# Two quarters of w loaded as f32 by SyncE's queue at the head of a matmul with batch normalization

## The chip, the cores and the metric

The kernel runs on one core of a Trainium2 chip. A core has TensorE for matmuls (PE in the profile, its weight loads PEld), VectorE (DVE), ScalarE (ACT), GpSimd (POOL) and SyncE (SP), and 16 DMA engines that serve the queues of all of them. The metric is the device time of one execution in microseconds. The kernel before took 205.82 us (median of three runs, 205.68 to 205.83).

## The reference

```python
batch, m, k, n = 16, 512, 1024, 768          # x: (16, 512, 1024), weight: (1024, 768), f32
y = np.matmul(x, weight)
mean = np.mean(y, axis=(0, 1), keepdims=True)
var = np.var(y, axis=(0, 1), keepdims=True)
y_norm = (y - mean) / np.sqrt(var + eps)
return (gamma * y_norm + beta).astype(np.float32)
```

A product of 8192 x 1024 by 1024 x 768, and then each of the 768 columns is normalized with its mean and variance over all 8192 rows. No column can be written before all rows of it have been multiplied.

## The kernel before, in words

The 8192 rows of x are 16 chunks of 512 (CH); a chunk is two pieces of 256 rows (QR). The 1024 of the contraction are four blocks jw of 256, and each block holds two (e = 0, 1) sets of 128. The 768 columns are six groups nt of 128; the first two are computed with rows on the partitions (rows_unit, matmul L510: x is the stationary operand), the other four with columns on the partitions (col_unit, matmul L575: w is the stationary operand).

x and w are f32 in HBM and bf16 in the matmuls. In the kernel before, both are cast on the way by GpSimd's DMA queue: load_x (L395, its DMA at L403) brings 256 or 512 rows into the tile "ring" in four DMAs, one for each 32 partitions; load_quarter (L386, L387) brings 32 partitions of w, for two blocks jw at once, into w_sb. A "quarter" i is such a group of 32 partitions; "the first pair of blocks" is jw 0 and 1, the second jw 2 and 3. VectorE then turns x in 32 x 32 squares (turn_x, L435 and L428) into xT_sb, which comes from the pool xtpool with 12 buffers.

The order of the loads is the list at L440: x's first 256 rows, w's first pair, x's second 256 rows, w's second pair, then the rest of x. BETWEEN (L262) moves two quarters of w's first pair ahead of x's first DMA (L401 and L402), so the queue of GpSimd runs: w quarters 0 and 1, x's first 256 rows (four DMAs), w quarters 2 and 3, x's second 256 rows, w's second pair, x further. A DMA of GpSimd's queue waits until the one eight places before it has landed, since eight semaphores go round.

At the very head SyncE's queue issues four tiny DMAs ("touched", L350), each of which reads one f32 word of 64 rows of w, for the four quarters of the first pair. Nothing computes with what they bring.

TensorE begins with WAKE = 8 f32 matmuls of 128 x 512 on a tile of zeros (wake, L587, matmul L591; each is two passes in the profile) and eight small ones (L594). Then it computes the first chunk in parts (part, L774, called at L780 to L787): with the first pair of blocks on the first 256 rows (8 matmuls L510 and 16 matmuls L575), one idle matmul (FILL = 1, L781 and L782), with the first pair on the second 256 rows, and then with the second pair on all 512 rows. The second chunk's rows follow.

All this work is written as tasks with an engine, an estimated duration and a due time; arrange (L122) plays them through with a model of the DMA queues (Wires, L98, whose field "free" is when the wires first come free) and gives the order in which each engine's instructions are emitted. Instructions emitted ahead of it, such as the four tiny DMAs, stand first in the order of their engine.

Of the kernel before, what the change touches and what calls it, by code (L numbers as in the profile page):

```python
# [97 lines left out]
class Wires:  # L98
# [2 lines left out]
    LANES = 8  # L101

    def __init__(self):
        self.free = 4.3
        self.lanes = {"SP": [], "POOL": [], "ACT": []}

    def ready(self, queue):
# [120 lines left out]
def kernel(  # L228
# [9 lines left out]
    nc = tc.nc  # L238
    f32 = mybir.dt.float32
# [5 lines left out]
    Kw, N = weight.shape  # L245
    assert K == Kw
    M = B * M0
    P = 128
# [6 lines left out]
    QPC = CH // QR  # L255
    JW = KQ // 64
    PIECES = ((0,QR),(QR,QR))
    WAKE = 8
    FILL = 1
    SMALL = 8  # L260
    TOUCH = 1
    BETWEEN = {0: [0, 1]}  # L262
    EARLY = 4
    SHORT = 2
    GA = 2
# [27 lines left out]
    def seq(bi):  # L293

        ins = bi.ins
        prev = last.get(ins.engine)
        if prev is not None:
            tc.add_manual_dep(
                ins, prev,
                mybir.DependencyInfo(mybir.DependencyClass.NoSync, mybir.DependencyReason.DATA),  # L300
                reason="order",
            )
        last[ins.engine] = ins.name
        return bi
# [39 lines left out]
    fss = singles.tile([P, 2], f32)  # L344

    seq(nc.scalar.activation(warm, eps_sb, AF.Sqrt))
    touched = singles.tile([P, 2, TOUCH], f32)
    first_rows = weight.rearrange("(i jw c e) n -> i c jw (e n)", i=4, jw=JW, e=2)
    for i in range(4):
        seq(nc.sync.dma_start(touched[32 * i:32 * i + 32, 0:2], first_rows[i, :, 0:2, 0:TOUCH]))  # L350


    tasks, turns = [], {}
# [93 lines left out]
    affine = None  # L447
    for kind, n, *n1 in order:
        if kind == "w":
            quarters = [i for i in range(4) if n > 0 or i not in sum(BETWEEN.values(), [])]  # L450
            took = len(quarters) * 192 * 4 * (n1[0] - n) / 4 * PER_KB * 1.024
            w_ready[n] = task(t, {"POOL": (0.535 * len(quarters), 0.535 * len(quarters))}, load_w(n, *n1, quarters), dma=took)
            w_ready[n].count = len(quarters)
            t += 2.1 * (n1[0] - n)
            if n1[0] == JW:
                idt = task(t, {"POOL": (0.6, 0.6)}, lambda eng: make_identity(nc, ident))
                task(t, act(0.25), lambda eng: seq(nc.scalar.copy(ident32, ident)), [idt])
            continue
# [319 lines left out]
            col_unit(nt, 0, jws, q0, q1)  # L778

    part(0, 1, [0, 1])  # L780
    fill_slot = Slot(banks)  # L781
    pe_task(0.87 * FILL, wake(FILL, fill_slot), [w_ready[0]], takes=[fill_slot])  # L782
    part(1, 2, [0, 1])
    for h in range(2):
        rows_unit(0, [2 * h, 2 * h + 1], [2, 3])
# [626 lines left out]
```

## Time and profile before

| What | Value |
|---|---|
| Time, median of three runs | 205.82 us |
| Span of the profiled execution, first to last instruction (the page gives no other time of it) | 204.07 us |
| Mean granted TensorE clock | 0.979 |
| Busy: PE, PEld, DVE, ACT, POOL | 189.3, 114.5, 159.3, 146.2, 124.1 us |
| First matmul with data | 12.14 us after the span's start |
| Last matmul of the product (L753) | ends at 186.6 us |
| Read from HBM, written to it | 36.7 MB, 25.2 MB |

The profile's page divides the span into 40 slices, one digit for the busy tenths of each engine in each. A view of waits sums, for each engine and line, the idle time ahead of an instruction and names what ended it. A view in order of time lists instructions with start and length in microseconds; an entry "x4" stands for four instructions merged. DMA issues have the engine name with a q ("SPq") or the engine's own name (POOL). Under a DMA instruction's tile names, "ring<-in_x_dram" is a load of x, "w_sb<-in_weight_dram" one of w. In the DMA part, q0 "software_dynamic" is GpSimd's queue and q1 "hardware_dynamic" that of SyncE. From issue to landing the eight DMAs of w take 6.2 us in the median, those of x's first pieces 5.9, the four tiny ones 2.6.

### The profile page before, as it was taken

How to read it: one execution, taken by the hardware profiler on the slowest of the kernel's cores; microseconds unless marked ns; L12 is line 12 of the kernel's file. 1: busy time of each engine (PE TensorE's matmuls, PEld its weight loads, DVE VectorE, ACT ScalarE, POOL GpSimd, SP SyncE). 2: the span in 40 equal slices, each digit the busy share in tenths (PEclk: the TensorE clock that was granted, in tenths of full speed). 3: DMA queues.
4: the chain of work that ended last, by engine and by line, in shares of the span. 5: the costliest groups of instructions: out<-in, count | busy, mean ns of one | idle time of the engine just before them, and what ended most of it. 6: DMA issues, size and time to landing. Idle time of an engine off the chain costs nothing.

```text
span 204.1 us, 3510 instructions
## 1 busy us (share of the span) xinstructions
PE 189.3 (93%) x1210; PEld 114.5 (56%) x1210; DVE 159.3 (78%) x250; ACT 146.2 (72%) x260; POOL 124.1 (61%) x150
## 2 busy tenths in 40 slices
PE   7969999999999999999999999999999999997900
PEld 3457554657488888777865444444444445544600
DVE  4031879999999999969989998987999878657900
ACT  2001461368989999899978766999998959956950
POOL 7776954877499989997403999389613312940000
PEclk9999999999999999999999999999999999999965
DMA  4999999999999999999686899899999999999998
GB/s 71 172 199 196 176 196 196 196 197 197 190 193 197 197 196 196 196 197 195 103 181 200 297 339 336 248 301 328 295 322 227 336 303 274 347 343 310 310 347 253
DMA packets 98562, 48.74 MB, mean 239 GB/s; under 512 B 24304, under 2 KB 98032, under 8 KB 98544
## 3 DMA queue, kind: packets, MB, share of 16 engines
q0 software_dynamic: 34624, 18.36, 65.5%
q1 hardware_dynamic: 63920, 30.16, 52.6%
q8 instruction: 9, 0.15, 0.3%
q14 instruction: 9, 0.07, 0.1%
HBM read 36.71 MB, written 25.17 MB: 303 GB/s over the span
## 4 chain that ended last, share of the span: by engine, by line
PE 86%; ACT 3%; DMA 3%; POOL 2%; issue 1%; ACTq 0%; DVE 0%; POOLq 0%
PE y_ps L575 54%; PE y_ps L510 24%; PE y_ps L814 4%; ACT o_sb L1361 3%; DMA ring<-in_x_dram 3%; PE o_ps L1044 1%; POOL ring L403 1%; POOL w_sb L387 1%; PE y_ps L753 1%; PE a_ps L903 1%; PE o_ps L1074 0%; ACTq L1407 0%; PE idle_ps L591 0%; PE tot_ps L871 0%; ACT ring L1252 0%
## 5 line engine op out<-in xcount | busy, mean ns | idle before, releaser
L575 PEld LDWEIGHTS <-w_sb 128*128 128x128 bf16 x520 | 50.3, 97 | 57.6
L575 PE MATMUL y_ps<-xT_sb,w_sb 128*128 128x512 bf16 (+1 forms) x272 | 59.3, 371 | 0.0
L575 PE MATMUL y_ps<-x_pl,w_sb 128*128 128x512 bf16 x248 | 57.4, 379 | 0.0
L403 POOL DMA_DIRECT2D ring<-in_x_dram x76 | 47.2, 626 | 14.4 <-DMA ring<-in_x_dram 5.5
L510 PE MATMUL y_ps<-w_sb,xT_sb 128*128 128x256 bf16 x448 | 50.6, 273 | 1.7 <-DMA ring<-in_x_dram 1.6
L510 PEld LDWEIGHTS <-xT_sb 128*128 128x128 bf16 x448 | 43.5, 98 | 9.4 <-DVE xT_sb L435 2.9
L435 DVE STREAM_TRANSPOSE xT_sb<-ring 128x1024 f32<-128x1024 f32 (+1 forms) x29 | 31.2, 1111 | 14.1 <-DMA ring<-in_x_dram 13.9
L711 DVE BATCH_NORM_STATS2 stats<-y_ps 128x6 f32<-128x512 f32 x46 | 30.9, 687 | 7.7 <-PE y_ps L575 7.2
L715 ACT CAST y_sb<-y_ps 128x512 bf16<-128x512 f32 x51 | 29.0, 593 | 10.4 <-DVE stats L711 6.3
L547 ACT COPY x_pl<-xT_sb 128x1024 bf16<-128x1024 bf16 x32 | 32.8, 1063 | 1.7 <-DVE xT_sb L435 1.7
L942 POOL TENSOR_TENSOR ring<-ring,sum 128x1024 f32<-128x1024 f32 (+1 forms) x11 | 23.8, 2188 | 14.9 <-ACT y_ps L724 10.9
L659 ACT ACTIVATE sq_sb<-y_ps 128x512 f32<-128x512 f32 x28 | 16.3, 610 | 16.2 <-PE y_ps L510 15.9
L666 POOL TENSOR_TENSOR sum<-sum,sq_sb 128x512 f32<-128x512 f32 x20 | 25.6, 1278 | 3.0 <-ACT sq_sb L659 1.7
L662 DVE TENSOR_TENSOR sum<-y_ps,sum 128x512 f32<-128x512 f32 x28 | 18.9, 675 | 6.3 <-ACT sq_sb L659 5.3
L672 ACT CAST y_sb<-y_ps 128x512 bf16<-128x512 f32 x28 | 16.3, 594 | 8.2 <-DVE sum L662 8.0
L1178 POOL TENSOR_TENSOR ring<-ring,sum 128x1024 f32<-128x1024 f32 x6 | 14.8, 2477 | 9.8 <-issue 8.5
L937 DVE TENSOR_TENSOR ring<-y_sb,a_ps 128x1024 f32<-128x1024 bf16 (+1 forms) x16 | 16.7, 1079 | 0.1
L1044 PE MATMUL o_ps<-ident,y_sb 128*128 128x128 bf16 x104 | 13.1, 221 | 1.6 <-DVE y_sb L1348 1.5
L1232 ACT CAST ring<-ring 128x1024 f32<-128x1024 bf16 x13 | 13.8, 1063 | 0.6 <-DMA ring<-y_sb 0.6
L1145 POOL COPY sum<-sum 32x256 f32<-32x256 f32 (+1 forms) x17 | 5.8, 340 | 13.4 <-DVE sum L1142 6.5
L428 DVE STREAM_TRANSPOSE xT_sb<-ring 128x2048 bf16<-128x2048 bf16 x6 | 13.5, 2290 | 0.1
L591 PE MATMUL idle_ps<-idle_sb 128*128 128x512 f32 x18 | 9.6, 688 | 1.5 <-DVE idle_sb L316 1.5
(104 smaller groups left out, 153.7 us busy)
## 6 DMA issues: line engine op xcount, KB each, us to landing
out_dram<-ring SPq DMA_DIRECT2D x37, 512.0 KB, 3.4
ring<-in_x_dram POOLq DMA_DIRECT2D x52, 256.0 KB, 8.8
out_dram<-o_sb SPq DMA_DIRECT2D x6, 512.0 KB, 4.7
ring<-in_x_dram POOLq DMA_DIRECT2D x16, 128.0 KB, 5.9
w_sb<-in_weight_dram POOLq DMA_DIRECT2D x8, 192.0 KB, 6.2
out_dram<-ring SPq DMA_DIRECT2D x6, 256.0 KB, 3.0
ring<-in_x_dram POOLq DMA_DIRECT2D x4, 192.0 KB, 7.8
out_dram<-o_sb SPq DMA_DIRECT2D x3, 256.0 KB, 2.5
```

Source lines behind the costliest of these rows:

```text
L403: bi = seq(nc.gpsimd.dma_start(x_bf[32 * i:32 * i + 32], src[:, :, KQ * i:KQ * (i + 1)]))
L435: seq(nc.vector.transpose(dst, src[:, :, jw0:jw1]))
L510: seq(nc.tensor.matmul(y_ps[:, s], x_of(c, jw, e, t * P, (t + 1) * P), w_sb[:, jw, e, 0:NA], start=(s == 0 and jw == 0 and e == 0), stop=( ...
L547: seq(nc.scalar.copy(dst, pairs) if eng == "ACT" else ENG[eng].tensor_copy(dst, pairs))
L575: seq(nc.tensor.matmul(y_ps, w_sb[:, jw, e, nt * P:(nt + 1) * P], moving(c, jw, e, q0 * QR, q1 * QR, parted), start=(jw == 0 and e == 0 an ...
L659: seq(nc.scalar.activation(sq_sb[:, 0:n], slot.tile[:, 0:n], AF.Square))
L662: seq(nc.vector.tensor_add(sum1, slot.tile[:, 0:n], sum1))
L666: seq(ENG[eng].tensor_add(acc, acc, state["sq"][:, 0:n]))
L711: seq(nc.vector.bn_stats(dst, slot.tile))
L715: seq(nc.scalar.copy(y(nt, c), slot.tile))
L937: seq(nc.vector.tensor_mul(slot.o, y_row[c].y[:, s0:s1], aff[0][:, None, :].to_broadcast([P, n, NA])))
L942: seq(ENG[eng].tensor_add(slot.o, slot.o, row[:, None, :].to_broadcast([P, n, NA])))
```

## The change

SyncE's queue now loads quarters 0 and 1 of w's first pair as f32, in four DMAs of 192 KB (two quarters by two blocks jw), into two tiles from xtpool. VectorE casts block 0 of both quarters into w_sb (64 partitions x 1536 elements), ScalarE block 1. These six instructions take the place of the four tiny DMAs, ahead of everything that the planner orders on these engines but behind the memsets on VectorE and the table load on ScalarE. GpSimd's queue no longer loads these two quarters and starts with x's first rows. The idle matmuls at the head are six instead of eight, the one between the two first parts is gone, and the planner's model has its wires free at 3.6 instead of 4.3.

```diff
@@ class Wires
     def __init__(self):
-        self.free = 4.3
+        self.free = 3.6
@@ constants
-    WAKE = 8
-    FILL = 1
+    WAKE = 6
+    FILL = 0
     SMALL = 8
-    TOUCH = 1
-    BETWEEN = {0: [0, 1]}
+    AHEAD = (0, 1)
+    BETWEEN = {}
@@ ahead of the planned work
-    touched = singles.tile([P, 2, TOUCH], f32)
-    first_rows = weight.rearrange("(i jw c e) n -> i c jw (e n)", i=4, jw=JW, e=2)
-    for i in range(4):
-        seq(nc.sync.dma_start(touched[32 * i:32 * i + 32, 0:2], first_rows[i, :, 0:2, 0:TOUCH]))
+    ahead = [xtpool.tile([P, 2, N], f32, tag="xT", name=f"ahead{jw}") for jw in range(2)]
+    w_words = weight.rearrange("(i jw c e) n -> i c jw e n", i=4, jw=JW, e=2)
+    for i in AHEAD:
+        for jw in range(2):
+            seq(nc.sync.dma_start(ahead[jw][32 * i:32 * i + 32], w_words[i, :, jw]))
+    near = slice(32 * AHEAD[0], 32 * AHEAD[-1] + 32)
+    seq(nc.vector.tensor_copy(w_sb[near, 0], ahead[0][near]))
+    seq(nc.scalar.copy(w_sb[near, 1], ahead[1][near]))
@@ the loads of w
-            quarters = [i for i in range(4) if n > 0 or i not in sum(BETWEEN.values(), [])]
+            quarters = [i for i in range(4) if n > 0 or i not in AHEAD]
@@ the first parts
     part(0, 1, [0, 1])
-    fill_slot = Slot(banks)
-    pe_task(0.87 * FILL, wake(FILL, fill_slot), [w_ready[0]], takes=[fill_slot])
+    if FILL:
+        fill_slot = Slot(banks)
+        pe_task(0.87 * FILL, wake(FILL, fill_slot), [w_ready[0]], takes=[fill_slot])
     part(1, 2, [0, 1])
```

The order of instructions on each engine is otherwise the same in both kernels, with one exception on GpSimd: two small instructions that build the identity stand between other DMAs than before.

## Prediction

> **What bounds the kernel now.** I read the busy row of TensorE by slices first, then its waits, then the order of time of the first 26 us, then what the DMA queues moved there.
>
> ```profile
> span 204.1 us, 3510 instructions
> ...
> PE   7969999999999999999999999999999999997900
> ...
> PEclk9999999999999999999999999999999999999965
> ```
>
> TensorE is busy at nine tenths or more from the fifth of 40 slices to the 37th. Its waits, all of them:
>
> ```profile
> PE y_ps L510 <- DMA ring<-in_x_dram: 1.6, 1, 1.6
> PE o_ps L1044 <- DVE y_sb L1348: 1.5, 1, 1.5
> PE idle_ps L591 <- DVE idle_sb L316: 1.5, 1, 1.5
> ```
>
> Between the wait at the head and the one at the tail TensorE never stands idle, so what moves the head earlier moves the end by as much, if the loads come earlier too. The head in order of time (start, length, engine, line, count, idle before):
>
> ```profile
> 0.74 1.81 SPq L350 DMA_DIRECT2D touched<-in_weight_dram  x4
> 1.30 1.21 POOL L387 DMA_DIRECT2D w_sb<-in_weight_dram  x2 [0.85 <-POOLq L1393]
> 1.49 8.63 PE L591 MATMUL idle_ps<-idle_sb 128*128 128x512 f32 x16 [1.49 <-DVE idle_sb L316]
> 2.51 2.29 POOL L403 DMA_DIRECT2D ring<-in_x_dram  x4
> 4.79 1.06 POOL L387 DMA_DIRECT2D w_sb<-in_weight_dram  x2
> 10.26 1.30 DVE L435 STREAM_TRANSPOSE xT_sb<-ring 128x512 f32<-128x512 f32 x2 [7.13 <-DMA ring<-in_x_dram]
> 12.14 1.03 PE L510 MATMUL y_ps<-w_sb,xT_sb 128*128 128x256 bf16 x8 [1.58 <-DMA ring<-in_x_dram]
> 14.83 1.02 PE L591 MATMUL idle_ps<-idle_sb 128*128 128x512 f32 x2
> 14.85 1.30 DVE L435 STREAM_TRANSPOSE xT_sb<-ring 128x512 f32<-128x512 f32 x2 [3.28 <-DMA ring<-in_x_dram]
> ...
> 18.61 1.91 PE L510 MATMUL y_ps<-w_sb,xT_sb 128*128 128x256 bf16 x16
> ...
> 24.62 1.25 DVE L435 STREAM_TRANSPOSE xT_sb<-ring 128x1024 f32<-128x1024 f32 x1 [0.69 <-DMA ring<-in_x_dram]
> ```
>
> Beside these lines I put the trace's semaphore records, which tell when the last of a transfer's 16 parts landed. w's quarters 0 and 1: 4.99 and 6.02. The four parts of x's first 256 rows: 8.09, 8.77, 9.51, 10.14. w's quarters 2 and 3: 11.06 and 12.00. x's second 256 rows: 14.73 (last part). w's second pair of blocks: 18.47. x's fourth 256 rows: 24.50. So TensorE begins four times at a landing: at 12.14 (0.14 after w's quarter 3; the turn of x, done by about 11.0 for the half needed, had been there), at 15.85 (x turned by 15.5, then the tail of the idle matmul), at 18.61 (landing 18.47, and TensorE itself free at 18.53), at 25.93 (landing 24.50, turn to 25.87, TensorE free at 25.89). The name "ring" in the wait of 1.58 is that of a later transfer on the same semaphores.
>
> The stream itself is what these landings wait for. In the first 2.6 us only the hardware queue moved anything (packets, MB, share of 16 engines):
>
> ```profile
> q1 hardware_dynamic: 160, 0.00, 3.2%
> ```
>
> and afterwards the DMA engines are full except in one stretch (columns: length, busy time of PE, PEld, DVE, ACT, POOL, granted clock, DMA share, GB/s):
>
> ```profile
> 5.00:6.00 1.00, 1.00 (x3) 0.38 (x2) 0.00 (x0) 0.00 (x0) 1.00 (x4) 1.00 1.15 152
> 6.00:7.00 1.00, 1.00 (x4) 0.43 (x3) 0.00 (x0) 0.00 (x1) 0.92 (x4) 1.00 0.82 91
> 8.00:9.00 1.00, 1.00 (x3) 0.38 (x2) 0.00 (x0) 0.00 (x0) 0.57 (x1) 1.00 1.37 206
> ```
>
> Against 206 GB/s the two stretches before lost 0.26 + 0.56 us, and 7 to 8 (180 GB/s) another 0.13: about 0.95 us soon after x is first read.
>
> **The change, part by part.** The order of the instructions on each engine is the same in both kernels but for what follows.
>
> *Start of the stream.* SP's first DMA is issued at 0.74 and its first packet runs at 1.75; its second transfer's first packet at 2.22. POOL's first DMA, issued at 1.30, has its first packet at 2.69 (packet records). Now SP's four transfers carry w's quarters 0 and 1, so payload flows from 1.75 instead of 2.69: 0.94 us earlier. POOL's first issue, still at 1.30, is x's (x's first packets at about 2.69 in place of 5.2).
>
> *Work of the stream.* To the landing of w's quarter 3 each DMA engine has 8 packets of quarters 0 and 1, 64 of x, 8 of quarters 2 and 3, before and after. A packet of a cast quarter reads 6,144 bytes and takes 247 ns; a quarter adds 0.92 to 0.96 us to the landings, a 128 KB part of x 0.63 to 0.74. A packet of 6,144 bytes without cast is not in the trace. From the store packets (27 ns at 512 bytes, 46 at 1,024) a line gives 46 + 5,120/512 x 19 = 236 ns; from the code loads (8,192 bytes in 309, 16,384 in 945) 232 to 354. I take 240, next to the cast packet with the same read: sum 0. Bounds: 8 x (232 - 247) = -0.1 us, 8 x (354 - 247) = +0.86 us. Both queues share the 16 engines packet by packet: the third touch, 4 packets on each engine, landed at 5.16 beside the 4 packets of w's quarter 0, at 4.99. So SP's 6 KB packets are not held up by x's 512-byte ones; at 1.75 + 8 x 0.247 + a few of x's + 0.3 from last packet to landing, quarters 0 and 1 are in at about 4.7.
>
> *First packets.* The first twelve of POOL's queue took 460 to 992 ns, most over 800, instead of 247: about 0.6 us. It may hit x's first packets now, or w's, or both: I take once, as before. Bounds: 0 and +0.7. The slow stretch of 0.95 us I also keep: it came right after x's first read, and x is still first read. Bounds: it vanishes under w's packets (-0.95), or stays.
>
> The sum at the stream: -0.94 + 0 + 0 + 0, so w's quarter 3 at about 11.05 instead of 12.00, and every later load by as much, since POOL's order behind it is the same transfers and each still waits for one that lies eight back and landed earlier.
>
> The Trainium skill (DMA: Bandwidth & Descriptors, "Issuing engines are not separate DMA queues") says that DMAs of all issuers run on the same 16 engines, and that spreading them saves only the issue time. By that, the gain is what POOL no longer issues ahead of x, the row of 1.21 us, and the sum would be -1.2 in place of -0.94; the records of the two queues' first packets give the smaller one, which I use.
>
> *The two casts.* DVE casts 64 partitions x 1,536 elements ahead of its first turn; nearest rows: L547's DVE copy (1,024 in 715 ns) and L435's transpose (1,024 in 1,224), so 1.07 to 1.84 us. ACT the same size: L547's copy on ACT, 1,024 in 1,063, so 1.6 us. From 4.7 both end by 6.6. Behind DVE's wait stand the turns of x's first rows, whose data land at about 9.2; behind ACT's stands the copy of ident (0.30 us, at 7.00 before), whose first reader is past 100 us. The two f32 tiles hold two of the x pool's twelve buffers; the tiles that take these next wait for SP's transfers too, some 30 us after they landed. SP itself has nothing to issue until gamma, which lands from 53 us. Cost 0, covered by some 2.5 us; if w's f32 rows landed after 7.4, DVE's part beyond it would reach the first turn, and only what exceeds w's quarter 3 (1.9 us after x) the first matmul.
>
> *Fewer idle matmuls.* Two of eight at the head are four passes of 0.43 us, off a stretch that nothing waits for: with the eight small ones behind them they end near 8.84 instead of 10.56 (9.95 + 0.61 in the order of time). The one between the parts (1.02 us) ends at 15.85 where x was turned from 15.5: up to 0.3 us, but the third begin, bound by a landing, takes it back. Cost 0, and no gain of its own.
>
> *Carried on.* With 0.95: first matmul 11.2, first part (2.7 us) to 13.9; x's second rows land at 13.8 and are turned by 14.6, so the second part runs 14.75 to 17.45; w's second pair lands at 17.5, the third begin at 17.65 (18.61 before); the fourth at 24.95 (25.93), x's fourth rows landing at 23.55. Behind it TensorE has no wait until the tail. The sum is -0.95 against the span of 204.07. The timed runs lie 1.75 us above that span (205.82), which the change does not touch: 204.87, say 204.9.
>
> **Rivals.**
>
> *The packets are dear.* The 354 ns end: -0.94 + 0.86, nothing left: 205.7. For it: large packets are the slowest row per byte there is. Against: those are code, and the cast's packet reads as much in 247. Chance 0.15.
>
> *The stretch vanishes.* x's first reads lie under w's packets and the 0.95 us at 5 to 8 us is saved too: 203.9. For it: two queues then fill the engines. Against: one slow packet holds both queues' work on its engine (the third touch waited). Chance 0.10.
>
> *The clock.* TensorE stands idle from 8.84 to 11.2, 2.4 us instead of 1.58; the granted clock stayed at 1.00 over the 1.58. If it falls, the first passes show the price: 0.85 us each instead of 0.43 until 4.2, so 2.7 us at half rate, 1.4 us lost. The first part then ends at 15.3, the second at 18.0, 0.35 past the third landing: 205.2. The Trainium skill (TensorE: Matmul & The Clock Gate, "Why this matters for your kernels") draws the line at idle gaps over about 3 us, which this stays under by little. Chance 0.05.
>
> *First reads of w stall: slower.* The four touches read a word of every row of w's first pair at 1.75 to 4.7. They go, and quarters 2 and 3 are first read in the middle of the stream, quarters 0 and 1 by SP's own packets. Each first read may cost what the first packets cost, 0.6 to 0.7 us: three of them are +2.1, less 0.94: 207.0; two: 206.3; say 206.6. It decides from two stalls on. For it: the slow first packets, and the slow stretch at x's first read. Against: w's quarters 0 and 1 were slow though touched, and neither x's later rows nor w's second pair show a dip (186 to 218 GB/s from 11 to 21 us). Chance 0.16.
>
> **How the numbers follow.** The forecast, 204.4 to 205.4, has 0.54 and is the likeliest, so 204.9. Cut where 0.16 lies above (the stalls) and some 0.04 below (the vanished stretch), the range is 204.0 to 206.3. A measurement of this kernel tells 0.2%, 0.41 us, from no change: faster means under 205.41. Forecast, clock, vanished stretch and a sliver of the dear packets: 0.69. Same, nearly all of it the dear packets: 0.15. Slower, the stalls: 0.16.
>
> **What would show it.** Packets of 6,144 bytes on the hardware queue from 1.75, some 240 ns each, done before 5; the casts over by 7; w's quarter 3 landing near 11.05 and the first L510 matmul near 11.2; the begins that were at 18.61 and 25.93 about 0.95 earlier, with no new wait of TensorE later. Wrong if those packets take over 300 ns, if a second slow stretch shows where quarters 2 and 3 flow, if the granted clock falls under 1.00 near 10 us, or if the head gains and a later load takes it back.

## The result, and the profile after

The changed kernel took 208.40 us (median of four runs, 207.56 to 209.23) against 205.82 (205.68 to 206.06) of the kernel before: 1.012 times as long, 95% interval 1.009 to 1.0151. Its profiled execution took 208.61 us, with a span of 206.8. The forecast was 204.9 us, in a range up to 206.3, so the change went the other way.

The page of the changed kernel, from its first two parts (span, busy tenths of TensorE in 40 slices, granted clock in tenths):

```profile
span 206.8 us, 3486 instructions
...
PE   7779999999999999999999999999999999996500
...
PEclk9969999999999999999999999999999999998855
```

The clock row has a 6 in the third slice that the row of before does not have. TensorE's waits, all of them (line, what ended the wait, us in total, times, longest):

```profile
PE y_ps L514 <- DMA w_sb<-in_weight_dram: 2.6, 1, 2.6
PE o_ps L1049 <- DVE y_sb L1353: 1.5, 1, 1.5
PE idle_ps L595 <- DVE idle_sb L316: 1.5, 1, 1.5
```

No wait was added in the middle, and the wait at the tail is the same. The head in order of time (start, length, engine, line, operation, count, idle before):

```profile
0.74 1.80 SPq L351 DMA_DIRECT2D ahead<-in_weight_dram  x4
1.29 2.45 POOL L407 DMA_DIRECT2D ring<-in_x_dram  x4 [0.85 <-POOLq L1398]
1.49 7.35 PE L595 MATMUL idle_ps<-idle_sb 128*128 128x512 f32 x12 [1.49 <-DVE idle_sb L316]
...
7.12 0.95 DVE L353 CAST w_sb<-ahead 64x1536 bf16<-64x1536 f32 x1 [3.98 <-DMA ahead<-in_weight_dram]
7.66 1.47 ACT L354 CAST w_sb<-ahead 64x1536 bf16<-64x1536 f32 x1 [5.42 <-DMA ahead<-in_weight_dram]
...
8.67 0.61 PE L598 MATMUL idle_ps<-idle_sb 128*128 128x128 bf16 x8
...
9.96 1.30 DVE L439 STREAM_TRANSPOSE xT_sb<-ring 128x512 f32<-128x512 f32 x2 [1.89 <-DMA ring<-in_x_dram]
...
11.86 1.54 PE L514 MATMUL y_ps<-w_sb,xT_sb 128*128 128x256 bf16 x8 [2.58 <-DMA w_sb<-in_weight_dram]
...
13.20 3.13 PE L579 MATMUL y_ps<-xT_sb,w_sb 128*128 128x256 bf16 x16
...
18.86 1.91 PE L514 MATMUL y_ps<-w_sb,xT_sb 128*128 128x256 bf16 x16
```

The first matmul comes at 11.86 instead of 12.14: 0.28 us of the 0.95 forecast. Its eight take 1.54 us instead of 1.03, because the granted clock was 0.50 from 12.24 to 15.65, and the begin that was at 18.61 is at 18.86. Yet the product's last matmul ends at 186.50, 0.12 us before that of the kernel before (186.62). The head thus ends about even, and the 2.6 us are lost behind it.

The tail shows where. SyncE's last stores in the kernel before, from the view in order of time (the length is from the first issue to the last one's end):

```profile
189.31 10.56 SPq L1364 DMA_DIRECT2D out_dram<-o_sb  x11
```

and in the changed kernel:

```profile
189.20 12.84 SPq L1369 DMA_DIRECT2D out_dram<-o_sb  x11
```

The same eleven stores take 2.3 us more. ScalarE's last copy ends at 196.7 and 196.9 in the two, and the DMA engines work on until the last store lands: 203.15 before, 205.90 after. In the semaphore records the six stores of 512 KB land 1.50 us apart before; after, the last three of them land 1.63 to 1.85 after the one ahead. The windows show the same (length, busy time of the five engines, clock, DMA share, GB/s); before:

```profile
98.00:110.00 12.00, 12.00 (x99) 8.93 (x97) 10.75 (x31) 10.04 (x31) 1.53 (x5) 1.00 0.58 123
195.00:203.00 8.00, 0.00 (x0) 0.00 (x0) 0.00 (x0) 1.67 (x3) 0.00 (x0) 0.54 1.11 333
```

after:

```profile
98.00:110.00 12.00, 11.95 (x98) 8.90 (x98) 10.76 (x31) 10.18 (x31) 1.50 (x5) 1.00 0.78 110
195.00:203.00 8.00, 0.00 (x0) 0.00 (x0) 0.00 (x0) 1.86 (x3) 0.00 (x0) 0.60 1.03 289
```

The engines are as busy as before, but the DMA moves 289 GB/s instead of 333 in the store stretch, and between 98 and 110, where the transposing DMAs begin, it is busy for 0.78 instead of 0.58 and moves less. SyncE's queue in that stretch (packets, MB, share of 16 engines), before:

```profile
q1 hardware_dynamic: 5280, 1.31, 48.5%
```

after:

```profile
q1 hardware_dynamic: 4740, 1.18, 69.6%
```

Ten per cent fewer packets take nearly half as much time again. Over the whole run the 256-byte packets of the transposes add up to 31.7 us a DMA engine, where they were 24.3 (in other traces with the buffers where they were, up to 28.6). Nothing in the diff touches these DMAs. What the diff does touch is a tile of 8 bytes a partition: "touched" goes, it filled 32 bytes in the first pool, and every pool behind it (xtpool with the buffers of x and of the last outputs, o_sb; then y, squares) now begins 32 bytes lower: xtpool at 66,528 bytes instead of 66,560, which is 130 x 512. The tile "ring", from which most of the stores leave, stands ahead of "touched" and did not move. In the changed kernel SyncE's queue runs 674 to 709 packets a microsecond from 186 us to 194, while the last stores from "ring" land (by 192.91) and the first, smaller ones from o_sb; from 194 on, with the stores of 512 KB from o_sb, it runs 551 to 602. Why the smaller stores from o_sb do not pay (they land 0.34 to 0.78 us apart, as before) no run shows.

### The profile page after: what moved, and what is told of

It reads as the page before. It is cut to its first block, busy times and chain, and to the rows that moved or that the text cites. A ratio compares the mean times of both kernels' runs of the same rounds, so it can differ in the third digit from the quotient of the medians.

```text
span 206.8 us, 3486 instructions
## 1 busy us (share of the span) xinstructions
PE 187.9 (91%) x1189; PEld 116.2 (56%) x1204; DVE 158.8 (77%) x251; ACT 147.3 (71%) x261; POOL 122.8 (59%) x148
## 4 chain that ended last, share of the span: by engine, by line
PE 85%; DMA 4%; ACT 3%; POOL 1%; issue 1%; ACTq 0%; DVE 0%; POOLq 0%
PE y_ps L579 53%; PE y_ps L514 24%; DMA w_sb<-in_weight_dram 4%; PE y_ps L819 4%; ACT o_sb L1366 2%; PE o_ps L1049 2%; POOL ring L407 1%; PE y_ps L757 1%; PE a_ps L908 1%; PE o_ps L1079 0%; ACTq L1412 0%; PE tot_ps L876 0%; ACT ring L1257 0%; POOL w_sb L391 0%; DVE y_sb L1353 0%
## 5 line engine op out<-in xcount | busy, mean ns | idle before, releaser
L579 PEld LDWEIGHTS <-w_sb 128*128 128x128 bf16 x520 | 51.1, 98 | 58.0
L579 PE MATMUL y_ps<-x_pl,w_sb 128*128 128x512 bf16 x241 | 56.7, 379 | 0.4
L439 DVE STREAM_TRANSPOSE xT_sb<-ring 128x1024 f32<-128x1024 f32 (+1 forms) x29 | 31.1, 1110 | 8.8 <-DMA ring<-in_x_dram 8.6
L715 DVE BATCH_NORM_STATS2 stats<-y_ps 128x6 f32<-128x512 f32 x46 | 30.3, 685 | 3.6 <-PE y_ps L579 3.4
L719 ACT CAST y_sb<-y_ps 128x512 bf16<-128x512 f32 x51 | 28.7, 593 | 5.8 <-DVE stats L715 3.0
L676 ACT CAST y_sb<-y_ps 128x512 bf16<-128x512 f32 x28 | 16.1, 600 | 7.8 <-DVE sum L666 7.4
L1179 DVE TENSOR_TENSOR ring<-r_sb,a_ps 128x1024 f32<-128x1024 bf16 x6 | 7.3, 1222 | 6.5 <-DMA out_dram<-ring 5.8
```

What stands on the lines that cost most here:

```text
L439: seq(nc.vector.transpose(dst, src[:, :, jw0:jw1]))
L579: seq(nc.tensor.matmul(y_ps, w_sb[:, jw, e, nt * P:(nt + 1) * P], moving(c, jw, e, q0 * QR, q1 * QR, parted), start=(jw == 0 and e == 0 an ...
L715: seq(nc.vector.bn_stats(dst, slot.tile))
L719: seq(nc.scalar.copy(y(nt, c), slot.tile))
```

## Experiments

"Time from the last matmul" below means from the end of the product's last matmul to the landing of the last store: 16.53 us before, 19.40 after. Every run has its own runs of the kernel before beside it; their medians lie between 205.8 and 206.1.

### Where the buffers lie

**The changed kernel with 32 bytes put back.**

```diff
-    tmp = singles.tile([P, NT], f32)
+    tmp = singles.tile([P, NT + 8], f32)
```

> The changed kernel with tmp made 32 bytes longer, so that the buffers of x, y and the squares stand again at multiples of 512 bytes in each partition, as before the change; nothing else. Theory A (the shift of these buffers by 32 bytes, from the tile of 8 bytes that went, makes transposing DMAs and stores slower): about 205.6 us, last store landed near 203.1 after the span's start, the 512 KB stores of the tail 1.50 us apart to the end. Theory B (the loss is the half clock and the head): stays at 207.5 to 209, tail stores up to 1.85 us apart. Theory C (other buffers for x, not their address): stays as B.

Measured: 206.51 us (204.85 to 207.49, ten runs), ratio 1.001 (0.9982 to 1.0038). Last six big stores 1.50 us apart again; time from the last matmul 16.57.

**The kernel before with the same edit**, which moves its buffers 32 bytes up.

> The kernel before with tmp made 32 bytes longer, so that its buffers stand 32 bytes off; nothing else. Theory A: 207.5 to 209 us, with the head (first matmul 12.14, L757-like last matmul near 186.6) as before and the loss in the transposing DMAs from 100 us on and in the tail. Theories B and C: 205.8, no change.

Measured: 208.41 us (208.24 to 208.94), ratio 1.0125 (1.0104 to 1.0145). Transposes 30.5 us an engine, the last three big stores 1.81 to 1.83 apart, time from the last matmul 19.13; the head is that of the kernel before. So 32 bytes alone make the kernel before as slow as the changed one, and giving them back takes nearly all the loss away.

**One part at a time.** In the kernel before, a one-word tile is moved from the first pool into a pool of its own between the x buffers and the y buffers:

```diff
     xtpool = ctx.enter_context(tc.tile_pool(name="xtpool", bufs=XT))
+    gap = ctx.enter_context(tc.tile_pool(name="gap", bufs=1))
...
-    warm = singles.tile([P, 1], f32)
+    warm = gap.tile([P, 1], f32)
```

With this alone the x and output buffers lie 32 bytes lower and y where it was; with "NT + 8" too, x is in place and y (with the squares) 32 bytes higher.

> The kernel before with the tile warm moved from the first pool to a place of its own behind the pool of x: the twelve buffers of x (which also hold the last blocks' outputs) stand 32 bytes off, those of y and of the squares where they were. If the shift of the output tiles makes the last stores slow: the last 512 KB stores 1.84 instead of 1.50 us apart, four of them, +1.0 to +1.4: 206.9 to 207.3; the 256-byte packets of the transposing DMAs as before (24 us summed over packets, divided by 16 engines). If only y counts: 205.9.

> The counterpart: the buffers of x in their place, those of y (which the transposing DMAs read, and whose buffers also take the raw turns) and of the squares 32 bytes off. If the transposes suffer: their packets 30 to 32 us instead of 24 to 28, last stores 1.50 us apart, +1.3 to +1.7: 207.2 to 207.6. If only the output tiles count: 205.9. The two shifts together should come near the 2.5 of the run with both.

Measured, x and output moved: 208.27 us (207.99 to 209.18), ratio 1.0108 (1.0087 to 1.013). The tail of this kernel in order of time:

```profile
190.06 12.48 SPq L1365 DMA_DIRECT2D out_dram<-o_sb  x11
```

The long store series is there, landings 1.86 apart, and the transposes are as before (24.4 us). Measured, y moved: 207.20 us (206.65 to 207.76), ratio 1.0064 (1.0042 to 1.0086), with stores 1.50 apart and transposes at 31.1. So the output buffers' place sets the stores' rate, and y's place that of the transposes, which read y. The two losses (2.2 and 1.3 us by the ratios) add up to more than both moves at once cost (2.6); why is not shown.

**How fine the step is.** The kernel before with its buffers moved by 64 bytes ("NT + 16") and by 256 ("NT + 64"):

> The kernel before with all three pools 64 bytes off instead of 32. If what counts is a line of 64 bytes: 205.9, transposes and last stores as before. If it is 512 bytes (or anything above 64): 207 to 208.5, as with 32.

> The kernel before with the tile tmp made 256 bytes longer, so that the buffers of x and the output, of y and of the squares all lie 256 bytes on from where they were; nothing else. Theory G256 (a DMA pays for a start that is not a multiple of 256 bytes): as the kernel before, 205.6 to 206.2, packets of the transposing DMAs 24 to 25 us in sum over 16, last stores 1.50 us apart. The Trainium skill (DMA: Bandwidth & Descriptors, "How a descriptor splits into AXI transactions") says that a transaction must start at a multiple of 256 bytes, which is this theory. Theory G512 (the start must be a multiple of 512): as with shifts of 32 and 64 bytes, 207.5 to 209, transposes 30 to 32, stores 1.8 apart. If only the transposes or only the stores mend, 206.6 to 208.

Measured: 209.11 us with 64 bytes (208.38 to 210.41, ratio 1.0153, 1.0093 to 1.0213), with the last stores 1.75 to 1.86 apart and transposes at 31.4. With 256 bytes 205.96 us (205.62 to 206.71), ratio 1.0 (0.9982 to 1.0018), transposes 24.4 and this store series:

```profile
189.57 10.66 SPq L1364 DMA_DIRECT2D out_dram<-o_sb  x11
```

My expectation of a 64-byte line fell, and a start at a multiple of 256 bytes (not 512) is enough. This is what the Trainium skill states (DMA: Bandwidth & Descriptors, "How a descriptor splits into AXI transactions"): a transaction must start at a multiple of 256 bytes, and for a packet that starts elsewhere the first one begins at the multiple below and fetches bytes that nobody uses. The runs agree with that granule as far as they go (32 and 64 bytes off pay, 256 does not; 128 was not tried). They do not agree with the page's count of beats: an estimate by it gives a 512-byte packet 32 bytes above a multiple 17 beats instead of 16 and one 32 bytes below 23, while both were measured alike (1.83 and 1.86 us a store, 1.22 and 1.24 times the 1.50).

**What the tail is made of.** The table sorts all traces by the time from the last matmul; the last column counts the packets of SyncE's queue in the second microsecond after that matmul.

| Traces | Time from the last matmul | Packets |
|---|---|---|
| 13 of the 15 with these buffers at multiples of 256 bytes | 16.53 to 16.77 us | 310 to 439 |
| The other two: without the tiny DMAs, and the last version below | 17.62 and 18.14 | 683 and 679 |
| y moved | 17.12 | 684 |
| x and output moved | 19.08 | 320 |
| All moved (the changed kernel, 32 and 64 bytes) | 19.13 to 19.40 | 691 or 692 |

In the 13 the queue has caught up with its stores when the product ends, and the end follows the last matmul, wherever between 185.55 and 196.08 us that is. Two things lengthen the tail: stores left over when the product ends (about 680 packets, a full queue, and 0.6 to 1.6 us), and slow stores from o_sb.

### The idle matmuls and the clock

**The changed kernel with the 32 bytes and the idle matmuls of before.**

```diff
-    WAKE = 6
-    FILL = 0
+    WAKE = 8
+    FILL = 1
```

> The changed kernel with the 32 bytes restored and the idle matmuls as before (eight at the head, one between the parts). Theory A with a clock that falls for want of idle matmuls: granted clock 1.00 from the first matmul on, the second pair of blocks of the first chunk begins near 18.4 instead of 18.86, time equal to the run with the 32 bytes alone or up to 0.3 us below it. If idle matmuls do not hold the clock: 0.5 again near 12 to 15 us and the same begin.

Measured: 205.67 us (204.67 to 206.06, ten runs), ratio 0.9986 (0.9972 to 1.0001). Its window from 10 to 16 us, and below it that of the same kernel with six idle matmuls (the first experiment):

```profile
10.00:16.00 6.00, 6.00 (x43) 4.05 (x42) 2.61 (x4) 0.30 (x1) 4.48 (x10) 1.00 1.25 203
```

```profile
10.00:16.00 6.00, 3.87 (x21) 2.79 (x22) 2.51 (x4) 0.30 (x1) 4.51 (x10) 0.72 1.25 203
```

In the second, TensorE was granted 0.50 from 12.55 to 15.96, after an idle stretch of 2.69 us. Its third begin is at 19.12, and at 18.39 with eight. The medians of the two differ by 0.84 us, though the intervals of their ratios overlap. The single runs of the one with six spread over 2.6 us, of the one with eight over 1.4, and the mean granted clock of each run parts the former: six of the ten have 0.965 to 0.972, which no timed run of the kernel before and none of the one with eight has (0.973 or more), and took 205.81 to 207.49 us (median 206.59); the other four have 0.985 or more and took 204.85, 205.16, 205.28 and 206.52.

**The kernel before with six idle matmuls and none between the parts.**

> The kernel before with the changed kernel's idle matmuls (six, none between the parts); w still comes by GpSimd's queue. If the clock falls for want of idle matmuls: idle from about 8.9 to 12.1, granted clock 0.5 for 3.4 us, the first part at 4.1 instead of 2.7 us, the third begin 0.3 to 1.5 us after 18.61, 206.1 to 207.3 us. If they are worth nothing: 205.8.

Measured: 205.95 us (205.66 to 206.96), ratio 0.9998 (0.998 to 1.0016). Its profiled run is the longest, 206.96, and has the clock at 0.50 from 13.04 to 16.45, after an idle stretch of 2.76 us. By their mean clock (0.964 to 0.972) six of the ten runs had it, as far as that tells; they took 205.66 to 206.96, the other four 205.67 to 206.35, so here it cost little. In all these traces the clock changes at steps of 3.41 us whose phase differs from run to run (the first full clock began between 4.37 and 7.58). In the changed kernel the step from 8.83 to 12.24 held 0.83 us of matmuls, and the next was granted 0.50; in the two kernels here it was 0.72 and 0.65. An idle stretch of 2.15 us in the run with 64 bytes, cut by the edge of a step, left the clock at 1.00. The Trainium skill (TensorE: Matmul & The Clock Gate, "Why this matters for your kernels") puts the danger at gaps of over about 3 us; here 2.58 to 2.76 were enough.

### Why the stream's lead was lost

SyncE's packets of 6,144 bytes started at 1.79, about as forecast, but took 350 ns in the median and 394 in the mean instead of 240 (in the packet records), and its last load landed at 7.57 instead of 4.7. The 0.28 us gained at the first matmul is itself not far from the scatter: the nine kernels with the head of before (one of them with fewer idle matmuls, one without the tiny DMAs) have it at 11.97 to 12.93, and this head at 11.86, 12.13 (32 bytes back) and 11.92 (idle matmuls too).

**Quarters 2 and 3 in place of 0 and 1**, with 32 bytes and the idle matmuls of before:

```diff
-    AHEAD = (0, 1)
+    AHEAD = (2, 3)
```

> The changed kernel with the 32 bytes restored and the idle matmuls as before, but with quarters 2 and 3 of w (partitions 64 to 127) on SyncE's queue, and 0 and 1 on GpSimd's. Theory P (SyncE's packets are slow since they and x's first two parts, which come at the same time, write into the same half of the partitions): SyncE's loads landed by about 6.3 instead of 7.6, the last quarter of w near 11.0 instead of 11.8, third begin near 17.8 instead of 18.4, time about 205.0. Theory R (slow because the memory is read there for the first time, or because f32 writes twice the bytes anywhere): as with quarters 0 and 1, 205.7.

Measured: 205.96 us (205.39 to 206.34), ratio 0.9997 (0.9984 to 1.001); mean packet 381 ns, last SyncE load at 7.59, against 389 and 7.75 in the same kernel with quarters 0 and 1. By these, meeting x's first rows in the same partitions is not what made them slow, though the median fell from 367 to 283 ns.

**GpSimd's queue later**, by six small memsets ahead of its first DMA, again with 32 bytes and the idle matmuls of before:

```diff
+    for spare in (tot[:, 0], tot[:, 1], stats[:, 0:80, 0], stats[:, 0:80, 1], tot[:, 0], tot[:, 1]):
+        seq(nc.gpsimd.memset(spare, 0.0))
```

> The changed kernel with its buffers put back (32 bytes more in tmp) and the idle matmuls as before, and with six small memsets on GpSimd ahead of its first DMA, so that x's first packets come some 2 us later and SyncE's f32 packets run alone at first. Theory B (those packets are slow because GpSimd's packets of x run beside them): median under 300 ns, the last of SyncE's loads landed by 5.5. Theory O (they are slow of themselves, or for what else happens at the start): median over 300 ns, landed after 6.5 as in the changed kernel (7.57). The slow stretch of the stream that ended near 7 us in all kernels: if it belongs to a time after the start it stays at 5.5 to 7 us, if to the first packets of GpSimd's queue it ends near 9. Time 205.5 to 207.0 by B, 206.5 to 207.5 by O, since x is late by up to 2 us in either and only the amount that the stream loses differs.

Measured: 205.62 us (205.33 to 206.53), ratio 0.9987 (0.9968 to 1.0006). The memsets held x back less than meant: its first packet came at 4.35 instead of 3.11. Mean packet 380 ns; while they ran alone, from 3 to 4.5 us, the median was about 460 and the 16 engines moved 196 KB a microsecond. They are slow by themselves. The slow stretch of the stream stayed in its place (221 KB read from 5 to 6 us, 207 in the changed kernel); with a delay of 1.24 us that speaks against x's first packets as its cause and does not rule them out.

**All partitions at once.** SyncE brings block 0 of all four quarters in one DMA over 128 partitions (three tiny DMAs behind it keep the count of four and the buffers in place), GpSimd block 1; idle matmuls as before. The second kernel brings the same block in four DMAs of 32 partitions:

```diff
+    ahead = xtpool.tile([P, 2, N], f32, tag="xT", name="ahead")
+    seq(nc.sync.dma_start(ahead, w_words[:, :, 0]))
+    seq(nc.vector.tensor_copy(w_sb[:, 0, 0], ahead[:, 0]))
+    seq(nc.scalar.copy(w_sb[:, 0, 1], ahead[:, 1]))
...
-                load_quarter(i, jw, jw1)
+                load_quarter(i, jw or 1, jw1)
```

> The changed kernel with the idle matmuls as before and the buffers in place, where SyncE brings another half of w's first pair, as many bytes: block 0 of all four quarters in one DMA over 128 partitions (quarters 0 and 1 were 64 partitions), and three tiny DMAs behind it so that its queue counts four as before; VectorE and ScalarE cast 768 elements on 128 partitions each, GpSimd's queue brings block 1. Theory D (the f32 packets are slow because 16 DMA engines write into the ports of one half of the partitions' groups): packets of 6,144 bytes 234 to 300 ns in the median, all landed by 5.5; the 0.7 us of lead is kept in part, first matmul 11.2 to 11.7, time 204.6 to 205.6. The Trainium skill (SBUF - State Buffer, "Door 1: The DMA port swizzle") says that partitions 0 to 63 reach only eight of 16 ports and 128 reach all, which is this theory. Theory O (the start of the stream is slow whatever it carries): packets over 350 ns in the median, landed after 6.5, time as the changed kernel with idle matmuls and buffers as before, 205.3 to 206.0.

> The same half of w's first pair (block 0 of all four quarters), casts and GpSimd's queue as in the kernel with one DMA over 128 partitions, but brought by SyncE in four DMAs of 32 partitions, one quarter after the other. Theory D (ports): in each DMA only a few ports are written, so packets as slow as in the changed kernel, 350 to 470 ns in the median, the last landed after 6.5, time 205.2 to 206.2. Theory O: as the one DMA over 128 partitions. If it is quick (under 300 ns) while that one is too, what helped is not the partitions but the smaller share of a row, and D falls.

Measured: the first 215.40 us (ratio 1.0456). It could not answer the question: its packets trickled in until 16 us, in its window

```profile
11.00:14.00 3.00, 0.00 (x0) 0.00 (x0) 0.00 (x0) 0.00 (x0) 0.00 (x0) 1.00 0.26 82
```

the DMA share is 0.26, that is about four of 16 engines at work, as many as the source's outer steps (four quarters of 32 rows); each of the tiny DMAs behind it, too, has four of its 16 parts landing after 15 us and the others before 8.2. The second, in four DMAs, took 207.33 us (206.97 to 208.68, ratio 1.0084): mean packet 349 ns, and a first matmul at 11.49, but now eight DMAs stand on GpSimd's queue ahead of x's second rows where the changed kernel has six, and the second part began at 16.70 instead of 15.68. Its median packet of 255 ns is under the 350 to 470 that I expected by theory D. Neither settles the packets.

**Two hardware queues.** SyncE's queue brings quarter 0, ScalarE's queue, ahead of its table load, quarter 2; in the control, quarter 1. Both have the 32 bytes, the idle matmuls of before and a cast for each quarter and block:

```diff
-    AHEAD = (0, 1)
+    AHEAD = (0, 2)
...
+    for jw in range(2):
+        for i in AHEAD:
+            eng = nc.scalar if i == 2 else nc.sync
+            seq(eng.dma_start(ahead[jw][32 * i:32 * i + 32], w_words[i, :, jw]))
+    seq(nc.scalar.activation(warm, eps_sb, AF.Sqrt))
```

> The changed kernel with buffers in place and the idle matmuls as before, but SyncE's queue brings quarter 0 (partitions 0 to 31) and, at the same time, ScalarE's queue quarter 2 (64 to 95), two DMAs each, and the casts are four. Theory D (16 engines writing f32 into one half of the partitions get some 210 KB/us together, which is 464 ns a packet; by the Trainium skill, SBUF - State Buffer, "Door 1: The DMA port swizzle", partitions 0 to 63 share eight ports and 64 to 127 the other eight): packets of 6,144 bytes under 300 ns in the median, since both halves are written at once. Theory O (the early stream is slow whatever it writes): 350 to 460 ns, as with quarters 0 and 1.

> The control of the one before: the same two queues, but quarters 0 and 1 (partitions 0 to 31 and 32 to 63), all in one half. Theory D: 400 to 480 ns in the median, well above the one before. Theory O: the same as the one before, whatever that is. If both are under 300, it was the single queue that made them slow.

Measured: median packet 239 ns with quarters 0 and 2, 459 with 0 and 1 (means 338 and 416). ScalarE's queue on the two pages (packets, MB, share of 16 engines), first quarter 2:

```profile
q10 hardware_dynamic: 96, 0.39, 0.5%
```

then quarter 1:

```profile
q10 hardware_dynamic: 96, 0.39, 0.8%
```

On this queue the same packets and bytes take over half as much time again when both quarters lie in one half of the partitions. SyncE's queue hardly shows it in the mean (404 and 417 ns), because with quarters 0 and 2 fourteen of its first sixteen packets took over 700 ns. From 3 to 4 us, when both queues run, they move 412 KB a microsecond with quarters 0 and 2 and 246 with 0 and 1. So the price is at least in part one of place once more: 16 engines that write f32 into one half got 196 (above) to 246 KB a microsecond. By the Trainium skill (SBUF - State Buffer, "Door 1: The DMA port swizzle") partitions 0 to 63 reach eight of the 16 ports; the pair of runs agrees. It is one execution of each (the last version below, with quarters 0 and 1 again, has a median of 466 ns and 270 KB), and place does not explain the median of 283 with quarters 2 and 3, which lie in one half too. The cast packets of a quarter write 3,072 bytes in 247 ns, which for 16 engines is 199 KB a microsecond as well; whether the same limit holds them is not shown.

The times of the two: 205.97 us (204.83 to 206.90, ratio 1.0002, 0.9981 to 1.0023) and 205.61 (204.87 to 206.94, ratio 0.9984, 0.9958 to 1.0011). Both profiled executions are the lowest of their ten; in the control the order of time has

```profile
10.96 1.03 PE L516 MATMUL y_ps<-w_sb,xT_sb 128*128 128x256 bf16 x8 [0.41 <-DMA w_sb<-in_weight_dram]
```

With the dear packets the lead came in full there, 1.18 us at the first matmul, so packet price is not all of it. The records of the 16 parts of a landing show the rest. w's last needed quarter landed from 10.62 (first engine) to 12.01 (last) before; from 9.93 to 11.73 after; and from 9.97 to 10.83 in the control. In the changed kernel the middle engine was 0.58 us ahead of before, the last one 0.28. The bytes read by 12 us can't tell: they are 3,134 KB before, 3,323 after and 3,396 in the control, but 2,978 in the kernel before moved by 256 bytes, whose first matmul came at 12.01. TensorE waits for the last engine. What puts the engines out of step is not shown: the 16 parts of this landing lie 1.80 to 2.56 us apart with quarters on one hardware queue (seven traces, without the one DMA over 128 partitions), 0.74 to 1.19 with two (three traces), but with w on GpSimd's queue alone, where no such packet runs, 0.82 to 2.12 (nine). With two queues the lead also reached the end in both traces: the product ended 1.07 and 1.03 us earlier than before, the last store landed 1.03 and 1.00 earlier. The medians of ten runs do not show that much.

**One queue, both halves in turn** (quarters 0 and 2, block by block, with four casts; 32 bytes and idle matmuls as before):

> The changed kernel with buffers in place and the idle matmuls as before; SyncE's queue alone brings quarters 0 and 2 in turn (quarter 0 block 0, quarter 2 block 0, quarter 0 block 1, quarter 2 block 1). Theory D: between 250 and 400 ns in the median, as far as the engines drift apart in their packets, time 205.2 to 205.8. Theory O: 350 to 460 ns, time 205.4 to 206.0.

Measured: median packet 248 ns, mean 342, but 205.97 us (205.06 to 206.74), ratio 0.9992 (0.9972 to 1.0011). Cheaper packets in the median, and no gain: w's last quarter landed from 10.07 to 12.15, a spread of 2.08 us where the control has 0.86.

### The tiny DMAs

**The kernel before without them**, buffers kept in place by "NT + 8":

> The kernel before without the four tiny DMAs, its buffers kept in place by 32 bytes more in tmp. Theory S (my rival of the stalls: a first read of a part of w costs some 0.6 us of the stream, which the tiny DMAs took beforehand): w's quarter 3 lands 0.6 us or more later than 12.0, the first matmul at 12.7 or later, 206.4 or more. Theory N (they do nothing for the stream): quarter 3 at 11.8 to 12.1, first matmul 11.9 to 12.3, 205.6 to 206.1.

Measured: 207.22 us (206.63 to 207.54), ratio 1.0057 (1.0038 to 1.0076). But w's quarter 3 landed at 11.98, the first matmul came at 12.11 and the product's last ended at 186.66, all as before: no first read stalled. The time from the last matmul is 17.62 instead of 16.53. From about 153 us on, stores and transposes run 0.6 to 1.6 us behind those of the kernel before, and SyncE's queue is still full when the product ends.

**The same DMAs reading other rows** (the second pair of blocks):

```diff
-        seq(nc.sync.dma_start(touched[32 * i:32 * i + 32, 0:2], first_rows[i, :, 0:2, 0:TOUCH]))
+        seq(nc.sync.dma_start(touched[32 * i:32 * i + 32, 0:2], first_rows[i, :, 2:4, 0:TOUCH]))
```

> The kernel before with its four tiny DMAs reading the first word of the rows of w's second pair of blocks in place of the first pair: as many DMAs on SyncE's queue, as many packets, the same tile. Left open by the kernel without them: it took 1.2 us more, although its first matmul (12.11) and its last matmul of the product (186.66) stood where they were. Theory R (a first read of these rows matters): as without them, 206.9 to 207.5, last matmul to last landing 17.3 or more. Theory C (what matters is that SyncE's queue has four DMAs more, so that all later DMAs of this queue stand elsewhere in it): as the kernel before, 205.6 to 206.3, last matmul to last landing 16.5 to 16.8. Nothing of the head moves by over 0.2 us in either.

Measured: 205.88 us (205.47 to 206.58), ratio 0.9991 (0.9976 to 1.0006), time from the last matmul 16.53. Which rows they read does not matter; that they are there does. That it is their number on SyncE's queue fits both runs, but not the two profiled runs with two hardware queues: those have two DMAs at the head of SyncE's queue, and 16.58 and 16.55 us from the last matmul. Why they matter, and by what the queue's later DMAs lose, is open. The changed kernel has four DMAs in their place.

### A version quicker than both

The control with two hardware queues has two DMAs on SyncE's queue. Two tiny DMAs behind them bring the count to four, and their tile takes the place of the 32 bytes:

```diff
+    touched = singles.tile([P, 2, 1], f32)
+    first_rows = weight.rearrange("(i jw c e) n -> i c jw (e n)", i=4, jw=JW, e=2)
+    for i in range(2):
+        seq(nc.sync.dma_start(touched[32 * i:32 * i + 32, 0:2], first_rows[i, :, 2:4, 0:1]))
```

> The kernel with quarters 0 and 1 on two hardware queues (SyncE's and ScalarE's, 205.61, single runs from 204.87 to 206.94), with two tiny DMAs behind SyncE's, so that this queue counts four as in the kernel before. Theory C (the later DMAs of SyncE's queue lose time where their count is not that of before): the runs above 206 vanish, median 204.8 to 205.3, a version quicker than both kernels. If the spread has another cause (the slowest DMA engine at the head, the clock): median 205.3 to 206.0, runs on both sides again.

Measured: 205.53 us (twelve runs; eleven from 205.28 to 205.68, one 206.96), against 205.82: ratio 0.9977 (0.9964 to 0.999). The median lies in the range that I gave for another cause (205.3 to 206.0), not in that of the count. Of the runs above 206, four of ten without the two tiny DMAs, one of twelve is left; that leans to the count and is too few to tell. The profiled run is the long one: its product ended at 185.74, 0.9 us before that of the kernel before, and its last store landed 18.14 us later, with SyncE's queue full when the product ended. What delays the stores in such a run stays open. At the head the lead was not used up: w's last needed quarter had landed at 10.97, and the first matmul came at 11.56, straight behind the eight idle matmuls, whose clock rose only at 6.86. So the idle matmuls that hold the clock can themselves stand in the way once the loads are quick.

## Why the prediction was wrong, point by point

**The step that failed: "what moves the head earlier moves the end by as much", carried to the sum by "Behind it TensorE has no wait until the tail".** For TensorE it held: from the begin of the second pair of blocks to the product's last matmul it is 167.6 to 168.6 us in every trace compared. But the sum took the 16.53 us behind that matmul along as they were, a term put at nothing without a reason. It measured 19.40: the product ended 0.12 us earlier than before, and the last store landed 2.75 later. The stores from o_sb were slower (1.63 to 1.85 us instead of 1.50), and so were the transposes ahead of them, so that the queue had not caught up when the product ended. I read TensorE's waits and the head, and not what runs in the last 16 us nor from which buffers. "The order of the instructions on each engine is the same in both kernels but for what follows" left out the one thing that the order can't show: the tile "touched" goes and all later buffers move by 32 bytes. Measured price: 1.9 us (208.40 against 206.51 with the bytes back) to 2.6 (the ratio of the kernel before with its buffers moved). No rival had it, and it is nearly the whole loss. With the buffers in place the rule did hold in 13 of 15 traces, whose tails are 16.53 to 16.77. A slip without weight: the row of TensorE has its nines from the fourth slice to the 36th; the 37th, with the wait at the tail, is a 7.

**"A packet of 6,144 bytes without cast ... I take 240".** The rows taken were stores, code loads and cast packets; none of them writes so many bytes at once into one half of the partitions. Measured 350 in the median, 394 in the mean; the upper bound of 354 was near the median. The rival "the packets are dear" was the right one for the head, and its +0.86 against the measured +0.67 (0.28 gained of 0.95) has about the right size, though the head's scatter (11.97 to 12.93 for the head of before) is as large. Also, what it lost was lost to the slowest of 16 engines: at w's last needed quarter the middle one was ahead by 0.58 us, the last by 0.28. In the sum, w's quarter 3 was to land at 11.05 and landed at 11.73.

**"First packets" and the slow stretch**, kept at once each: the stretch stayed (5 to 7 us in the changed kernel, too), its cause open. SyncE's first sixteen packets took 234 to 611 ns, x's first sixteen 59 or 60, from 3.11 us on where 2.69 was forecast; the longest packet of SyncE's took 1,382 ns, at 4.84 us.

**The two casts.** 0.95 us on VectorE and 1.47 on ScalarE, against 1.07 to 1.84 and 1.6 forecast. They began at 7.12 and 7.66, past 6.6, but the cover held: x's turn began at 9.96, when x had landed (9.84), and not later for the cast, which ended at 8.07.

**"Fewer idle matmuls ... cost 0".** This failed, by its own rival: the clock. The gap was 2.58 us where 2.4 was forecast, and the clock did fall, from 12.24 on, 0.38 us into the first part. The rival had the third begin 0.35 us past the landing; by the landing at 18.19 and the begin at 18.86 it was 0.67. In time it cost 0.5 us by the ratios of the two kernels with and without (1.001 and 0.9986, whose intervals overlap), 0.84 by their medians, and about 1.3 between the runs of one kernel with a low and a high mean clock (206.59 against 205.22). A chance of 0.05 was too low for a gap that near to the 3 us which the prediction itself named.

**"First reads of w stall: slower".** It had the sign by luck: without the tiny DMAs no load was later, and what lost time was the tail.

So by the ratios the change is: head about -0.3 us (0.9986, not told from nothing by its interval), idle matmuls about +0.5 (nor is this, by the ratios), buffers about +2.3 (1.012 against 1.001). These are the steps of one chain of kernels from before to after, so they add up to the 2.5 measured by construction.

## What to carry to other kernels

A tile added or removed is also an edit of every address behind it: before costing an edit, see which buffers move off a multiple of 256 bytes, and which DMAs with rows of 256 or 512 bytes read or write them. Read the end of the kernel as carefully as its head: if one engine's last work lies several microseconds ahead of the last landing, look whether the stores have caught up by then. If they have, the end follows that engine; if not, or if they become slower, the end is theirs. And a load priced by its reads must be priced by its writes too: how many bytes, and into which partitions at once.

## What the runs showed of the hardware that was not expected

- Stores of 512-byte rows from SBUF: 1.50 us for 512 KB from a multiple of 256 bytes, 1.63 to 1.88 for the last of them when 32 or 64 bytes off. Transposing DMAs with 256-byte packets: 24.0 to 28.6 us an engine against 30.5 to 31.7.
- f32 packets of 6,144 bytes: 459 and 466 ns in the median when two queues write into partitions 0 to 63, 239 when they write 0 to 31 and 64 to 95 (one execution each; 246 and 270 against 412 KB a microsecond from 3 to 4 us).
- A landing waits for the slowest of 16 DMA engines, and these were 0.74 to 2.56 us apart at w's last needed quarter.
- One DMA whose source rows come in four groups of 32 kept about four engines busy instead of 16 (share 0.26).
- Idle stretches of TensorE of 2.58 to 2.76 us were enough for a granted clock of 0.50 over 3.41 us.
- Four tiny DMAs fewer at the start of SyncE's queue cost 1.2 us at the other end of the kernel, for a reason not found.
